# Reciprocal square roots of a hybrid decoder layer: twelve VectorE steps against one VectorE step and a GpSimd power

## Chip, cores and metric

The kernel runs on one core of one Trainium2 chip. The metric is the device time of one execution in microseconds (us). Before the change three runs gave 2449.33, 2453.66 and 2454.43 us, so the median is 2453.66 us. The engines are called PE (TensorE), DVE (VectorE), ACT (ScalarE), POOL (GpSimd) and SP (the engine that starts most DMAs).

## What is computed

One layer for a prompt of 2048 tokens with 16 meta tokens ahead of it, and for 8 single tokens of running sequences. The parts that matter here:

```python
hn = rmsnorm(h, norm1_g)                       # rsqrt per token
q, f, i, g, a, b = split(hn @ w_in)
o, s_new = hgrn2_chunked(silu(q), 1 - f, i, log f)   # 4 heads, gated recurrence
y_hg = rmsnorm(o, hg_onorm_g) * silu(g)        # rsqrt per token and head
glu = a * sigmoid(b)
dw = depthwise_conv(glu, conv_w, 31 taps) + conv_b
y_cv = silu(layernorm(dw))                     # rsqrt per token
h = h + concat(y_hg, y_cv) @ w_out
h = h + square(relu(rmsnorm(h) @ w_up)) @ w_down
y = rmsnorm(h, final_g)                        # rsqrt per token
```

## The kernel before, in words

The prompt is worked on in four quarters of 512 tokens (the meta and sample tokens ride with the first). Every large product is done in three passes (`mm3`, high and low parts of both operands), in matmuls of 128 weights by up to 536 columns. Phase 1 runs, quarter by quarter, the input projection (24 units of 24 or 48 matmuls: columns a and b for the convolution, f, q, g, v for the heads) and the output projection (8 units). Phase 2 is the MLP over two halves. The weights of phase 1 are split into their parts once, by an ACT copy and a POOL subtraction (`split_to`), and are stored and loaded again later.

Beside these units run background tasks, written as Python generators: `x_pair` normalises and transposes two 128-token blocks of the input for the next quarter; `hgrn` does the recurrence of one head and quarter; `conv` starts two `conv_part` tasks for one 128-channel block, of which one adds taps on DVE into a PSUM bank and the other scales taps on ACT and adds them on POOL, until the 31 taps are used up, and the two sums are added; `ln` is the convolution's layer norm; `finish` and `finish_last` do the last norm. This two-sum convolution stands in the kernel before as well as after.

The order of all instructions is fixed when the program is built. `Model` keeps a clock for each engine, `Proxy.call` charges each instruction a cost (for a small DVE step of n elements 68 + 1.1 n ns, for POOL 60 + 2.2 n ns), and `Background.ready` lets a task issue its next step when by those clocks its input is there and the engine is free; for PE that is when the input is ready by the time PE comes to it. Each engine then runs its own list strictly in order and waits on semaphores. So where an engine is later than the planner's clock, whoever is next in line behind it waits.

`rsqrt` is called 49 times: once in `factors` (5 values for each partition), 6 times in `x_pair` (2), 16 times in `hgrn` (4), once in `hgrn_sample_norm` (32), 9 times in `ln_tiles` (2, once 1), 15 times in `finish` (1) and once in `finish_last` (2). All but the last 16 lie in phase 1. It is the bit trick with three Newton rounds: a multiply-add, a shift, an integer multiply-add, and nine more steps, all tiny, all on DVE, each needing the one before. `gap` adds 130 ns to the task's clock between two of them, so that other DVE work is put there. What follows a call: in `hgrn`, four ACT copies scaled by the result (into `on`, which is the tile `KPn`) and then four PE transposes of it; in `x_pair`, `row_bc`, which multiplies the identity by it on DVE (tile `dg`) for PE to spread; in `ln_tiles`, one more DVE step, an ACT normalisation into a `scr` tile and four PE transposes of that; in `factors`, the first two evictions.

In the trace `stat` and `kept` are the tiles of these small values. A row of DVE that writes `ps` from `glu` and `cw` is a convolution tap.

Of the kernel before, what the change touches and what calls it, by code (L numbers as in the profile page):

```python
# [10 lines left out]
I32 = mybir.dt.int32  # L11
U32 = mybir.dt.uint32
AF = mybir.ActivationFunctionType
ALU = mybir.AluOpType
AX = mybir.AxisListType

P = 128
# [11 lines left out]
HALO = TAPS - 1  # L29
DFF = 4096  # L30
EPS = 1e-6
MAGIC = float(0x5F3759DF)
INC = QT + META + NS
QOFF, FOFF, VOFF, GOFF, AOFF, BOFF = 0, 512, 1024, 1536, 2048, 2560

# [64 lines left out]
def _size(ap):  # L100
    n = 1
    for d in ap.shape[1:]:
        n *= d
    return n


class Proxy:
# [3 lines left out]
    def __getattr__(self, f):  # L111
        fn, name, model = getattr(self._eng, f), self._name, self._model

        def call(*args, **kw):
            out = kw.get("out", args[0] if args else None)
            if f == "dma_start":
                n = 4
                for d in out.shape:
                    n *= d
                model.dma(n)  # L120
            else:
                n = _size(out)
                if name == "pe":
                    rhs = kw.get("rhs")
                    if f == "transpose" or rhs.dtype != F32R:
                        cost = max(17 + 0.72 * n, 60.0) if f == "transpose" else max(1.67 * n, 214.0)
                        if n == 1:
                            cost = 425.0
                    else:
                        cost = 2.6 + 0.4167 * n  # L130
                elif name == "act":
                    cost = 130 + 0.8 * n
                    if not isinstance(kw.get("scale", 1.0), float):
                        cost += 100
                elif name == "pool":
                    cost = 60 + 2.2 * n
                elif f == "reciprocal":
                    cost = 60 + 6.3 * n
                elif f in ("bn_stats", "tensor_reduce"):
                    cost = 65 + 1.05 * _size(args[1])  # L140
                elif f in ("tensor_copy", "memset"):
                    cost = 65 + 0.53 * n
                else:
                    cost = 68 + 1.1 * n
                model.op(name, cost)
            return fn(*args, **kw)  # L146

        return call
# [71 lines left out]
def tile_hybrid_step(  # L220
# [6 lines left out]
    V, S, G, T, SP = (Proxy(e, n, model) for e, n in (  # L227
        (nc.vector, "dve"), (nc.scalar, "act"), (nc.gpsimd, "pool"), (nc.tensor, "pe"), (nc.sync, "dma")))
# [9 lines left out]
    def ct(shape, dt=F32, name=None):  # L238
        return const.tile(shape, dt, name=name)
# [8 lines left out]
    c0 = ct([P, HEADS], name="c0")  # L248
    nc1 = ct([P, HEADS], name="nc1")
    stat = ct([P, 104], name="stat")  # L250
    kept = ct([P, 88], name="kept")
    msn = ct([P, 2, 9], name="msn")
    rs2 = ct([P, 2, 9], name="rs2")
# [19 lines left out]
    ps = psum.tile([P, 8, 512], F32, name="ps")  # L273
# [11 lines left out]
    def sc(n):  # L285
        if scols[0] + n > 104:
            scols[0] = 0
        a = stat[:, scols[0]:scols[0] + n]
        scols[0] += n
        return a  # L290

    def keep(n):

        if kcols[0] + n > 88:
            kcols[0] = 0
        a = kept[:, kcols[0]:kcols[0] + n]
        kcols[0] += n
        return a

    def rsqrt(src, n, scale, parts=P, bufs=None):  # L300

        x, a, y = bufs or (sc(n)[:parts], sc(n)[:parts], keep(n)[:parts])
        V.tensor_scalar(x, src, scale, EPS, ALU.mult, ALU.add)
        yield from gap()
        V.tensor_scalar(a.bitcast(I32), x.bitcast(I32), 1, None, ALU.logical_shift_right)
        yield from gap()
        V.tensor_scalar(y.bitcast(I32), a.bitcast(I32), -1.0, MAGIC, ALU.mult, ALU.add)
        yield from gap()
        for _ in range(3):
            V.scalar_tensor_tensor(out=a, in0=x, scalar=-0.5, in1=y, op0=ALU.mult, op1=ALU.mult)  # L310
            yield from gap()
            V.tensor_tensor(a, a, y, ALU.mult)
            yield from gap()
            V.scalar_tensor_tensor(out=y, in0=a, scalar=1.5, in1=y, op0=ALU.add, op1=ALU.mult)
            yield from gap()
        return y

    def gap():
        model.cur.t += 130.0
        yield "dve"  # L320
# [21 lines left out]
    def bank1():  # L342
        got = yield from bank(1)
        return got[0]

    def until(*keys):
        while not all(k in done for k in keys):
            yield "poll"
        model.cur.t = max([model.cur.t] + [done[k] for k in keys])
# [9 lines left out]
    def mix_base(q):  # L359
        return K8 if q == NQ - 1 else 0  # L360

    def hi_lo(dst_hi, dst_lo, src):
        S.activation(dst_hi, src, AF.Copy)
        n = _size(src)
        if n >= 256 and max(model.t["pool"], model.t["pe"]) + 2.2 * n < max(model.t["dve"], model.t["pe"]) + 1.1 * n:
            G.tensor_tensor(dst_lo, src, dst_hi.bitcast(F32), ALU.subtract)
        else:
            V.tensor_tensor(dst_lo, src, dst_hi.bitcast(F32), ALU.subtract)
# [24 lines left out]
    def x_pair(q, pr):  # L393
        t0 = q * QT + pr * 256
        tiles = yield from take(xns, 2)
        yield "sp"
        for i, t in enumerate(tiles):
            SP.dma_start(t[:, 0:D], xp[t0 + i * P:t0 + (i + 1) * P, :])
        yield "act"
        ss = sc(2)  # L400
        for i, t in enumerate(tiles):
            S.activation(junk, t[:, 0:D], AF.Square, accum_out=ss[:, i:i + 1])
        yield "dve"
        r = yield from rsqrt(ss, 2, 1.0 / D)
        yield from row_bc([r[:, i:i + 1] for i in range(2)], bc_t[:, pr])
        yield from region(1, q - 1)
        left = [2]
        for w in range(2):
            bg.add(x_work(q, pr, w, tiles, left), 2.5)
# [146 lines left out]
    def factors(dgs, epilogues):  # L556

        n = META + NS
        yield from take1(dgate)
        yield "dve"  # L560
        r = yield from rsqrt(ss0, 5, 1.0 / D)
        for i in range(4):
            V.tensor_scalar(dgs[:, i], ident, r[:, i:i + 1], None, ALU.mult)
        V.tensor_scalar(dg_t[:n, 0, 0:n], ident[:n, 0:n], r[:n, 4:5], None, ALU.mult)
        yield "pe"
        b, b2 = yield from bank(2)
        for i in range(4):
            T.matmul(ps[:, b, i * P:(i + 1) * P], lhsT=ones, rhs=dgs[:, i], start=True, stop=True)
        T.matmul(ps[:, b2, 0:n], lhsT=ones[:n, :], rhs=dg_t[:n, 0, 0:n], start=True, stop=True)
        dgate.give(0)  # L570
        yield "act"
        S.activation(bc0[:, META:META + QT], ps[:, b, :], AF.Copy)
        S.activation(bc0[:, 0:META], ps[:, b2, 0:META], AF.Copy)
        S.activation(bc0[:, META + QT:INC], ps[:, b2, META:n], AF.Copy)
        banks.give(b, b2)
        done.add(("r0",))
        for i, f in enumerate(epilogues):
            yield "dve"
            f()
            done.add(("first", i))  # L580
# [205 lines left out]
    with tc.manual_schedule():  # L786
        make_identity(nc, ident)
        G.memset(ones, 1.0)

        with ExitStack() as p1:  # L790
            mix_p = p1.enter_context(tc.tile_pool(name="mix", bufs=1))

            def mt(shape, name, dt=F32):
                return mix_p.tile(shape, dt, name=name)
# [19 lines left out]
            aux = mt([P, 96], "aux")  # L814
# [62 lines left out]
            sqs = small[:, 320:352]  # L877
            dws = aux[:, 0:32].rearrange("p (c b) -> p c b", c=NC4)
            ms_ = aux[:, 64:96]
# [178 lines left out]
            def hgrn_sample_norm():  # L1058
                yield from until(*[("hs", h) for h in range(HEADS)])
                yield "dve"  # L1060
                V.tensor_tensor(sqs, osT, osT, ALU.mult)
                yield "pe"
                b = yield from bank1()
                T.matmul(ps[:, b, 0:32], lhsT=ones, rhs=sqs, start=True, stop=True)
                yield "dve"
                r_ = yield from rsqrt(ps[:, b, 0:32], 32, 1.0 / P, bufs=(aux[:, 32:64], sqs, ms_))
                banks.give(b)
                V.tensor_tensor(osT, osT, r_, ALU.mult)
                V.scalar_tensor_tensor(out=ms_, in0=osT, scalar=onorm, in1=sgs, op0=ALU.mult, op1=ALU.mult)
                yield "act"  # L1070
                for h in range(HEADS):
                    s_ = mix_base(0) + h
                    hi_lo(act[:, s_, 0, QT:QT + NS], act[:, s_, 1, QT:QT + NS], ms_[:, h * NS:(h + 1) * NS])
                done.add(("hsn",))
# [630 lines left out]
```

## Time and profile before

| what | before |
|---|---|
| median of three runs | 2453.66 us |
| the profiled execution, its own time | 2447.64 us |
| its span, first to last instruction | 2445.7 us |
| PE busy | 2352.7 us (96%) |
| DVE busy | 1171.4 us (48%) |
| ACT busy | 683.4 us (28%) |
| POOL busy | 520.7 us (21%) |
| mean granted TensorE clock | 0.982 |

The busy share is an average over two phases. PE is close to always busy after about 960 us, so only what happens before that, and the last 46 us, can move the time by much. There the question is which instruction PE waits for, and what that one waited for in its turn. The granted clock is given as a share of 2.4 GHz; 0.50 is the lower level, 1.2 GHz.

### The profile page before, as it was taken

The numbers are of one execution on the slowest core, as the hardware profiler recorded it, in microseconds if no ns is written. First come the engines' busy times: TensorE is split into PE (matmuls) and PEld (weight loads), VectorE is DVE, ScalarE is ACT, GpSimd is POOL, SyncE is SP. The second block draws the span as 40 slices with busy tenths as digits, with TensorE's granted clock in tenths as the row PEclk, the third lists the DMA queues.
The fourth block names the chain that finished last, engine by engine and source line by source line (L and its number), as shares of the span: only waits on it lengthen the run. The fifth ranks groups of instructions, "written<-read, shape, count | busy, mean of one in ns | idle before, by whom it ended". The sixth has DMA issues, their size and how long they took to land.

```text
span 2445.7 us, 31621 instructions
## 1 busy us (share of the span) xinstructions
PE 2352.7 (96%) x13000; PEld 2100.7 (86%) x13000; DVE 1171.4 (48%) x2003; ACT 683.4 (28%) x1239; POOL 520.7 (21%) x326
## 2 busy tenths in 40 slices
PE   8887898989999999999999999999999999999998
PEld 8887777967887788999999999999888888888887
DVE  6798978587659653523323323326722212222225
ACT  6443644463345333212212211213301100100112
POOL 4562414442237112222212212211000000000000
PEclk9889999999999999999999999999999999999999
DMA  9665454944474468644444444448522222222222
GB/s 300 201 215 175 153 192 139 307 165 167 168 248 159 144 233 294 232 155 141 130 150 135 138 147 140 136 153 304 216 94 95 94 98 92 98 92 98 92 93 97
DMA packets 159221, 396.27 MB, mean 162 GB/s; under 512 B 8772, under 2 KB 107657, under 8 KB 125278
## 3 DMA queue, kind: packets, MB, share of 16 engines
q1 hardware_dynamic: 158934, 394.00, 47.5%
q8 instruction: 102, 1.67, 0.3%
q14 instruction: 41, 0.34, 0.0%
q10 hardware_dynamic: 144, 0.26, 0.0%
HBM read 265.91 MB, written 128.79 MB: 161 GB/s over the span
## 4 chain that ended last, share of the span: by engine, by line
PE 73%; DVE 6%; ACT 1%; DMA 1%; issue 0%; POOL 0%; SPq 0%; ACTq 0%; POOLq 0%; DVEq 0%
PE ps L146 73%; DVE ps L146 3%; DVE stat L146 1%; ACT scr L146 0%; DVE kept L146 0%; DMA scr<-xscr 0%; DVE I L146 0%; DMA wsp<-kw 0%; POOL scr L146 0%; DVE act L146 0%; DVE scr L146 0%; DVE glu L146 0%; DVE B L146 0%; DVE xn L146 0%; ACT act L146 0%
## 5 line engine op out<-in xcount | busy, mean ns | idle before, releaser
L146 PE MATMUL ps<-act,wsp 128*128 128x512 f32 (+5 forms) x7704 | 1504.6, 354 | 8.8 <-POOL wsp L146 4.3
L146 PEld LDWEIGHTS ps<-act,wsp 128*128 128x128 f32 x7704 | 1284.4, 191 | 171.2 <-POOL wsp L146 4.9
L146 PE MATMUL ps<-hid,wsp 128*128 128x344 f32 (+4 forms) x3864 | 713.0, 345 | 1.6 <-DMA wsp<-kw 1.6
L146 PEld LDWEIGHTS ps<-hid,wsp 128*128 128x128 f32 x3864 | 646.4, 188 | 64.0 <-issue 1.8
L146 DVE TENSOR_TENSOR acc<-ps,acc 128x1032 f32<-128x1032 f32 (+5 forms) x160 | 162.0, 1013 | 467.4 <-PE ps L146 467.3
L146 POOL TENSOR_TENSOR wsp<-raw,wsp 128x1024 fp32r<-128x1024 f32 (+1 forms) x98 | 235.6, 2404 | 611.4 <-ACT wsp L146 575.8
L146 DVE TENSOR_TENSOR xn<-xn 128x1032 f32<-128x1032 f32 (+3 forms) x68 | 80.3, 1180 | 509.3 <-ACT hid L146 509.3
L146 ACT ACTIVATE xn<-ps 128x1032 f32<-128x1032 f32 (+5 forms) x74 | 69.2, 935 | 835.1 <-PE ps L146 832.3
L146 POOL TENSOR_TENSOR scr<-scr 128x512 f32<-128x512 f32 x172 | 227.8, 1325 | 266.8 <-ACT scr L146 241.8
L146 DVE SCALAR_TENSOR_TENSOR ps<-glu,cw,ps 128x512 f32<-128x512 f32 x292 | 219.5, 752 | 5.8
L146 ACT ACTIVATE wsp<-raw 128x1024 fp32r<-128x1024 f32 (+1 forms) x98 | 101.6, 1037 | 299.8 <-PE ps L146 216.0
L146 DVE TENSOR_TENSOR hid<-xn,hid 128x1032 fp32r<-128x1032 f32 (+3 forms) x68 | 133.5, 1963 | 2.3
L146 ACT ACTIVATE scr<-glu,cw 128x512 f32<-128x512 f32 x188 | 125.7, 715 | 2.0 <-DVE glu L146 2.0
L146 DVE TENSOR_TENSOR scr<-ps,scr 128x512 f32<-128x512 f32 x48 | 32.8, 684 | 81.1 <-DMA scr<-xscr 55.8
L146 ACT ACTIVATE hid<-xn 128x1032 fp32r<-128x1032 f32 (+3 forms) x68 | 69.0, 1015 | 2.2
L146 ACT ACTIVATE junk<-ps 128x128 bf16<-128x128 f32 (+3 forms) x100 | 38.3, 383 | 108.4 <-PE ps L146 95.2
L146 POOL TENSOR_TENSOR fg<-fg 128x512 f32<-128x512 f32 x28 | 36.6, 1307 | 97.7 <-ACT fg L146 97.7
L146 DVE RECIPROCAL I<-B 128x512 f32<-128x512 f32 (+1 forms) x16 | 54.0, 3378 | 0.5
L146 DVE SCALAR_TENSOR_TENSOR stat<-stat,kept 128x4 f32<-128x4 f32 (+4 forms) x144 | 41.8, 291 | 3.3
L146 DVE TENSOR_TENSOR act<-scr,act 128x512 fp32r<-128x512 f32 (+1 forms) x30 | 23.7, 791 | 37.7 <-ACT act L146 37.6
L146 PE MATMUL ps<-ident,scr 128*128 128x128 f32 (+1 forms) x148 | 22.1, 282 | 17.8 <-ACT scr L146 17.8
L146 DVE TENSOR_TENSOR stat<-stat,kept 128x4 f32<-128x4 f32 (+4 forms) x144 | 37.6, 261 | 3.4
(189 smaller groups left out, 1192.1 us busy)
## 6 DMA issues: line engine op xcount, KB each, us to landing
wsp<-kw SPq DMA_DIRECT2D x167, 1024.0 KB, 4.8
kw<-wsp SPq DMA_DIRECT2D x96, 1024.0 KB, 5.6
raw<-in_w_up_dram SPq DMA_DIRECT2D x32, 512.0 KB, 6.5
raw<-in_w_down_dram SPq DMA_DIRECT2D x32, 512.0 KB, 6.0
raw<-in_w_in_dram SPq DMA_DIRECT2D x24, 512.0 KB, 7.9
out_dram<-xn SPq DMA_DIRECT2D x18, 512.0 KB, 4.4
scr<-xscr SPq DMA_DIRECT2D x32, 256.0 KB, 7.2
hscr<-scr SPq DMA_DIRECT2D x32, 256.0 KB, 7.1
```

The costliest lines, as they stand in the source:

```text
L146: return fn(*args, **kw)
```

## The change

`rsqrt` becomes one DVE multiply-add (x = src · scale + EPS) and one POOL `tensor_tensor` with the operation power, whose second operand is a constant tile `mhalf` of -0.5. The eleven steps after the multiply-add are gone, and with them the twelve gaps into which other DVE work was put. The planner gets a cost for the new instruction. The sample norm writes to other scratch tiles. Nothing else is edited; but since the planner's clocks change, the order changes on every engine.

```diff
@@ Proxy.call
+                elif name == "pool" and ALU.pow in args:
+                    cost = 400 + 155 * n
                 elif name == "pool":
                     cost = 60 + 2.2 * n
@@ constants
+    mhalf = ct([P, 32], name="mhalf")
@@ rsqrt
-        x, a, y = bufs or (sc(n)[:parts], sc(n)[:parts], keep(n)[:parts])
+        x, y = bufs or (sc(n)[:parts], keep(n)[:parts])
         V.tensor_scalar(x, src, scale, EPS, ALU.mult, ALU.add)
-        yield from gap()
-        V.tensor_scalar(a.bitcast(I32), x.bitcast(I32), 1, None, ALU.logical_shift_right)
-        yield from gap()
-        V.tensor_scalar(y.bitcast(I32), a.bitcast(I32), -1.0, MAGIC, ALU.mult, ALU.add)
-        yield from gap()
-        for _ in range(3):
-            V.scalar_tensor_tensor(out=a, in0=x, scalar=-0.5, in1=y, op0=ALU.mult, op1=ALU.mult)
-            yield from gap()
-            V.tensor_tensor(a, a, y, ALU.mult)
-            yield from gap()
-            V.scalar_tensor_tensor(out=y, in0=a, scalar=1.5, in1=y, op0=ALU.add, op1=ALU.mult)
-            yield from gap()
+        yield "pool"
+        G.tensor_tensor(y, x, mhalf[:parts, 0:n], ALU.pow)
+        yield "dve"
         return y
@@ start of the schedule
         G.memset(ones, 1.0)
+        G.memset(mhalf, -0.5)
@@ hgrn_sample_norm
-                r_ = yield from rsqrt(ps[:, b, 0:32], 32, 1.0 / P, bufs=(aux[:, 32:64], sqs, ms_))
+                r_ = yield from rsqrt(ps[:, b, 0:32], 32, 1.0 / P, bufs=(aux[:, 32:64], ms_))
```

How the change moves instructions is seen in the engines' lists. The first place is DVE at the second head of the first quarter, where `rsqrt` works on 4 values. Before:

```order
L146 TENSOR_TENSOR V_123<-ps,fg 128x536
L146 TENSOR_SCALAR stat<-stat 128x4
L146 SCALAR_TENSOR_TENSOR ps<-glu,cw,ps 128x512
L146 TENSOR_SCALAR stat<-stat 128x4
L146 SCALAR_TENSOR_TENSOR ps<-glu,cw,ps 128x512
L146 TENSOR_SCALAR kept<-stat 128x4
L146 SCALAR_TENSOR_TENSOR ps<-glu,cw,ps 128x512
L146 SCALAR_TENSOR_TENSOR stat<-stat,kept 128x4
L146 SCALAR_TENSOR_TENSOR ps<-glu,cw,ps 128x512
L146 TENSOR_TENSOR stat<-stat,kept 128x4
L146 SCALAR_TENSOR_TENSOR ps<-glu,cw,ps 128x512
L146 SCALAR_TENSOR_TENSOR kept<-stat,kept 128x4
```

The same place now:

```order
L147 TENSOR_SCALAR ps<-glu,cw,vec 128x512
L147 SCALAR_TENSOR_TENSOR ps<-glu,cw,ps 128x512 x4
L147 TENSOR_SCALAR stat<-stat 128x4
L147 SCALAR_TENSOR_TENSOR ps<-glu,cw,ps 128x512 x2
L147 TENSOR_TENSOR Sg_123<-ps,fg 128x520
L147 SCALAR_TENSOR_TENSOR ps<-glu,cw,ps 128x512 x2
L147 SCALAR_TENSOR_TENSOR xn_90<-xn_91,smp,xn_90 128x128 x8
```

Before, a tap stood behind each of the twelve steps (six steps are shown, the other six go on in the same way). Now only the first step is left, and the taps stand in a row. The state update of the sample tokens (`xn` from `smp`, eight instructions) has come close behind it.

The second place is POOL, at the same head. Now:

```order
L147 TENSOR_TENSOR wsp_88<-raw_86,wsp_88 128x1024
L147 TENSOR_TENSOR scr<-scr 128x512
L147 TENSOR_TENSOR kept<-stat,mhalf 128x4
L147 TENSOR_TENSOR wsp_89<-raw_85,wsp_89 128x1024
L147 TENSOR_TENSOR scr<-scr 128x512
```

The power (`kept` from `stat` and `mhalf`) stands behind a weight split (`wsp`) and a convolution add (`scr`), and ahead of the next weight split.

The third place is PE between the last product with the state (`Sch`) of the third head of the third quarter and the transposes of its normalised output (`KPn`). Before:

```order
L146 MATMUL ps<-Sch,Q_117 128x128
L146 MATMUL ps<-act,wsp_87 128x512 x24
L146 MATMUL ps<-act,wsp_88 128x512 x3
L146 MATMUL ps<-ident,KPn 128x128 x4
L146 MATMUL ps<-ident,xn_92 128x128
```

The same place now:

```order
L147 MATMUL ps<-Sch,Q_119 128x128
L147 MATMUL ps<-act,wsp_88 128x512 x21
L147 MATMUL ps<-ident,KPn 128x128 x4
L147 MATMUL ps<-act,wsp_88 128x512 x3
L147 MATMUL ps<-act,wsp_89 128x512 x3
```

The transposes have moved forward: 21 matmuls of the projection stand ahead of them and not 27. Over the whole program the taps that DVE takes go from 292 to 299 and the POOL adds from 172 to 165.

## Rows read from the trace of the kernel before

**Rows 1.** Busy time by stage: PE, PEld, DVE, ACT, POOL, then granted clock, DMA.

```profile
0.00:420.00 420.00, 362.98 (x2256) 325.87 (x2257) 344.81 (x667) 211.45 (x452) 183.94 (x131) 0.93 0.59 197
420.00:960.00 540.00, 517.46 (x2712) 436.28 (x2711) 352.18 (x712) 228.42 (x481) 174.60 (x127) 0.98 0.60 208
960.00:2400.00 1440.00, 1437.94 (x7763) 1305.64 (x7762) 442.55 (x482) 230.66 (x269) 162.16 (x68) 1.00 0.41 137
```

**Rows 2.** Waits of PE, 0 to 960 us: total us, times, longest us.

```profile
PE ps L146 <- ACT KPn L146: 18.8, 5, 10.6
PE ps L146 <- ACT scr L146: 17.8, 5, 5.6
PE ps L146 <- DVE dg L146: 15.8, 5, 6.9
...
PE ps L146 <- POOL wsp L146: 4.3, 3, 2.0
```

**Rows 3.** Timeline, second head of the first quarter: start us, us, engine, instruction.

```profile
189.20 7.64 PE L146 MATMUL ps<-act,wsp 128*128 128x268 f32 x60
...
190.85 0.19 ACT L146 ACTIVATION_READ_ACCUMULATOR junk<-ps 128x1 f32 x1
...
194.33 1.09 DVE L146 TENSOR_SCALAR stat<-stat 128x4 f32<-128x4 f32 x1
...
197.94 2.34 POOL L146 TENSOR_TENSOR wsp<-raw,wsp 128x1024 fp32r<-128x1024 f32 x1
198.58 1.72 DVE L146 SCALAR_TENSOR_TENSOR stat<-stat,kept 128x4 f32<-128x4 f32 x1
200.22 0.74 DVE L146 SCALAR_TENSOR_TENSOR ps<-glu,cw,ps 128x512 f32<-128x512 f32 x1
...
206.84 0.16 DVE L146 SCALAR_TENSOR_TENSOR kept<-stat,kept 128x4 f32<-128x4 f32 x1
...
207.46 0.99 PE L146 MATMUL ps<-ident,KPn 128*128 128x128 f32 x3 [10.61 <-ACT KPn L146]
```

**Rows 4.** Timeline of PE: the first and the last of twelve long waits.

```profile
68.48 1.23 PE L146 MATMUL ps<-dg,ones 128*128 128x128 f32 x4 [6.95 <-DVE dg L146]
...
748.13 1.12 PE L146 MATMUL ps<-ident,scr 128*128 128x128 f32 x4 [4.40 <-ACT scr L146]
```

**Rows 5.** Busy time by stretch, just behind two of these waits (columns as above).

```profile
207.40:212.00 4.60, 4.54 (x21) 4.32 (x22) 4.38 (x9) 2.48 (x11) 2.56 (x2) 0.50 0.00 0
...
748.10:752.00 3.90, 3.87 (x12) 3.26 (x13) 3.64 (x5) 3.24 (x8) 0.46 (x1) 0.56 0.00 0
```

**Rows 6.** Timeline, third head of the third quarter, where nothing stands between the steps.

```profile
650.26 6.50 PE L146 MATMUL ps<-act,wsp 128*128 128x512 f32 x27
...
652.15 0.37 DVE L146 TENSOR_SCALAR stat<-stat 128x4 f32<-128x4 f32 x2 [3.91 <-ACT junk L146]
...
654.53 1.14 ACT L146 ACTIVATE KPn<-ps,kept 128x128 f32<-128x128 f32 x4 [2.41 <-DVE kept L146]
...
656.61 0.60 PE L146 MATMUL ps<-ident,KPn 128*128 128x128 f32 x4
```

**Rows 7.** Groups of DVE, 0 to 960 us: count, busy us, mean ns, idle before.

```profile
L146 DVE SCALAR_TENSOR_TENSOR stat<-stat,kept 128x4 f32<-128x4 f32 (+3 forms) x96 | 34.3, 357 | 2.2
...
L146 DVE TENSOR_TENSOR stat<-stat,kept 128x4 f32<-128x4 f32 (+3 forms) x96 | 30.1, 314 | 2.2
L146 DVE SCALAR_TENSOR_TENSOR kept<-stat,kept 128x2 f32<-128x2 f32 (+3 forms) x105 | 28.2, 268 | 2.6
...
L146 DVE SCALAR_TENSOR_TENSOR xn<-xn,smp,xn 128x128 f32<-128x128 f32 x32 | 11.7, 438 | 0.0
```

**Rows 8.** Groups of POOL, 0 to 960 us (columns as in the group before).

```profile
L146 POOL TENSOR_TENSOR scr<-scr 128x512 f32<-128x512 f32 x172 | 227.8, 1325 | 266.8 <-ACT scr L146 241.8 <-issue 12.7 <-DVE act L146 2.9
...
L146 POOL MEMSET ss<- 128x5 f32 x1 | 0.1, 104 | 0.0
```

**Rows 9.** Timeline of DVE, the last norm at the end of the program.

```profile
2436.98 0.17 DVE L146 TENSOR_SCALAR stat<-kept 128x2 f32<-128x2 f32 x1
...
2439.61 0.16 DVE L146 TENSOR_TENSOR kept<-kept,rs 128x2 f32<-128x2 f32 x1
```

More of the change, by code (lines that the diff above doesn't have):

```diff
@@ L31 @@
 EPS = 1e-6
-MAGIC = float(0x5F3759DF)
 INC = QT + META + NS
```

## The prediction, made before the changed kernel was run

> **What bounds the kernel now.** I read the busy time by stage first. From 960 to 2400 us PE is busy for 1437.94 of 1440 us at a granted clock of 1.00: nothing on another engine can shorten that stretch. From 0 to 960 us PE is busy for 362.98 + 517.46 = 880.4 us and idle for 79.6 us, and the granted clock is 0.93 and 0.98 [rows 1]. So the change can act there and in the last microseconds.
>
> Next I read whom PE waits for in that stretch. The three longest entries are the scaled copies of a head (`KPn`, 18.8 us), the tiles of the layer norm (`scr`, 17.8 us) and the diagonal of the input norm (`dg`, 15.8 us) [rows 2]. All three come directly behind `rsqrt`. Together they are 52.4 of the 79.6 us, in 15 waits, of which twelve are longer than 2 us (the timeline gives the first and the last of these twelve [rows 4]).
>
> Then I followed one such wait. The squares of the head end at 191.04 us. DVE begins the multiply-add only at 194.33 us, since it is working off its list, and finishes the last step at 207.00 us; PE has 7.64 us of other matmuls in the meantime and then idles for 10.61 us [rows 3]. The twelve steps take 12.7 us there because a tap of 0.74 us stands behind each of them, and because some are drawn out: one that reads two small tiles lasts 1.72 us and ends at 200.30 us, together with the POOL instruction that ends at 197.94 + 2.34 = 200.28 us [rows 3]. Where nothing stands between the steps, the whole chain takes 2.41 us, and PE, with 6.50 us of matmuls in hand, does not wait at all [rows 6].
>
> Behind a long wait PE also runs slowly for a while: 4.60 us at 0.50 (the 1.2 GHz level) after the wait of 10.6 us, 3.90 us at 0.56 after that of 4.40 us [rows 4, 5]. That is a loss of 4.60 · 0.50 = 2.3 us and of 3.90 · 0.44 = 1.7 us. I take 2.0 us for each of the twelve, 24 us in all.
>
> So the chains cost about 52 + 24 = 76 us of phase 1, and that is the most that shortening them can give back there.
>
> **What goes.** In phase 1 there are 32 calls on the small tiles. Three of the five kinds of step that go took 34.3 + 30.1 + 28.2 = 92.6 us of DVE in 297 instructions, of which 9 stay; the other two kinds add to that [rows 7]. So some 90 to 110 us of DVE work in phase 1 disappear. DVE is busy there for 344.81 + 352.18 = 697 of 960 us, and for 82% of the first 420 us [rows 1], and there it is late against the plan. The seven more taps that it now takes cost 7 · 0.74 = 5 us of that.
>
> **What comes.** Each call now waits for one POOL instruction. The trace has no power on POOL. From below, POOL's smallest row of a few columns is 0.10 us, and from above its longest is 2.34 us for 1024 columns [rows 3, 8]; I do not exclude more, which is a rival. The code of the change itself plans 400 + 155 n ns, that is 0.71 us for 2 values and 1.02 us for 4. I take 1.0 us for a head, which lies between the ends, and about 0.1 us for each hand-over.
>
> For a chain with nothing between its steps the new length at a head is: 652.15 - 650.26 = 1.9 us from PE's last state product to the multiply-add, 0.2 us for that, 0.1 + 1.0 + 0.1 us for the power, 0.4 us for the first scaled copy: 3.7 us. PE now has 21 and not 27 matmuls in hand, 21 · 6.50 / 27 = 5.1 us [rows 6]. That leaves 1.4 us, about one POOL add of 1.325 us [rows 8]. So the planner has used up part of the gain by asking for the result sooner: a chain behind one add is just in time, behind two it is late.
>
> **The sum**, against the profiled execution's own time of 2447.64 us:
>
> 1. The wait of 10.61 us. DVE begins its multiply-add no earlier than now, since the list ahead of it is as long. By the new order four taps, one eviction of the size of a tap and eight state updates of 0.44 us follow, 5 · 0.74 + 8 · 0.44 = 7.2 us [rows 3, 7], and PE wants these updates ahead of the transposes. They are done at 194.3 + 0.2 + 7.2 = 201.7 us; PE arrives at about 197.2 us. A wait of 4.5 us is left, 6 us are gained.
> 2. The other 41.8 us of chain waits. The step itself becomes 10 us shorter where taps stood in it, but the start is as late as DVE's list, and the consumers have moved forward. I take half as gained: 21 us.
> 3. The slow stretches behind them go with them, 24 · 27 / 52 = 12 us.
> 4. The 27 us of other waits of PE (79.6 - 52.4) are mostly on DVE, which loses some 90 us of work. I take 4 us as gained, with 0 and 15 us as ends.
> 5. POOL. Some 32 powers of 0.7 to 1.2 us and one on 32 values, 5.4 us by the plan's line, make about 33 us; seven adds of 1.325 us go. POOL is busy for 183.94 + 174.60 of 960 us [rows 1], so its share is no limit, but some nine powers stand ahead of a weight split. PE's waits for these splits are 4.3 us now [rows 2]; nine delays of 1.0 us would make at most 9 us more. I take 4 us lost, with 0 and 9 us as ends.
> 6. The end. From 2436.98 us to 2439.61 us DVE goes through the chain with nothing beside it but 0.5 us of other work: 2.6 us [rows 9]. Now it is 0.2 + 0.1 + 0.7 + 0.1 = 1.1 us, so 1.6 us less (rounded).
> 7. The 15 calls of the MLP phase lie beside PE's 1437.94 of 1440 us [rows 1] and count for nothing; if their cover were gone, they would cost what they cost before or less.
>
> Sum: -6 - 21 - 12 - 4 + 4 - 1.6 = -40.6 us, so 2407 us for an execution like the profiled one. That one is 6 us under the median of the runs shown, 2453.66 us; from the median the sum gives **2413 us**.
>
> GPSIMD Engine Reference in the Trainium skill, section "Instruction dispatch", says that the first call of freshly loaded code on that engine costs about 6 us without an instruction of its own; if that held for the power, the first call, ahead of the first evictions, would be later by that, and the sum would be 2419 us. No row of this trace shows it.
>
> **Rivals.**
>
> *Half of it comes back elsewhere.* While a POOL instruction runs, a small DVE step on SBUF tiles stays open until it ends, as the step of 1.72 us does, whereas a tap, which reads and writes PSUM, keeps its 0.74 us [rows 3]. The powers bring 33 us of POOL time of that kind. In addition DVE's lists are as tight as before, since the planner fills the freed time with taps. Then DVE remains late, the waits appear under other names (the state updates of item 1, the evictions), and of the 27 us of chain waits and the 12 us behind them about half is lost again: 2413 + 20 = 2433 us. For it speaks the wait of 4.5 us in item 1; against it, that 90 us of DVE work are gone for good. The same page of the Trainium skill, section "Specifications", states that the two engines share their SBUF interfaces and that DVE instructions with two SBUF inputs are among those that contend. By that rule this rival is real, and the step of 1.72 us agrees with it.
>
> *The power is the new wait, and the kernel is slower.* In the third head of the third quarter PE has 5.1 us in hand and the chain without the power takes 2.7 us. So from 2.4 us on, for the power with its place in POOL's line, every tight chain makes PE wait and drops its clock. With 4 us there are 32 waits of 1.6 us and 2.0 us of slow clock behind each: 32 · 3.6 = 115 us against the 76 us that go, 2453.7 + 39 = 2493 us. Even is 32 · (w + 2.0) = 76, so w = 0.4 us: 2.8 us for the power and its line. A power of 1.5 us behind one add of 1.325 us is already there. For it speaks that each POOL list holds adds that wait for ACT (241.8 us idle for that [rows 8]), so that a power can stand behind a late add; against it, that POOL is idle for 63% of phase 1.
>
> *Nothing measurable.* The planner moves each consumer forward by as much as the chain becomes shorter, and the lateness of DVE, which causes the waits, stays. Then only the end is gained: 2452 us. The order at the third place speaks for it, the 10 us by which an interleaved chain shrinks against it.
>
> **How the numbers follow.** The forecast gets 0.60, with 2385 to 2428 us as its own range: 2413 less half of items 2 and 3 again plus items 4 at its far end, and plus half of them. Half of it gets 0.20 (2428 to 2447 us), nothing measurable 0.08, slower 0.12. A measurement of this kernel can tell about 0.2%, 5 us, from no change. Faster is 0.60 + 0.20, same 0.08, slower 0.12. The range that leaves out the last two cases is 2382 to 2447 us; its lower end is close to the case in which all 76 + 1.6 us go (2376 us).
>
> **What would show it.** Right: PE's idle time from 0 to 960 us near 50 us, the three entries behind `rsqrt` near 25 us together, a power of 4 values near 1.0 us, the chain at the end shorter by 1.6 us, the stretch from about 960 us on as long as before. Half of it: new entries for `xn`, evictions or `act` in PE's waits. Slower: PE waiting for `KPn` in nearly all 16 heads, ACT waiting for POOL `kept`. The forecast is wrong if the entries behind `rsqrt` stay near 50 us, or if they go and the time stays.

## The result, and the profile after

| what | before | after |
|---|---|---|
| median of the runs beside each other | 2454.05 us (4 runs) | 2411.14 us (4 runs, 2407.99 to 2413.44) |
| the profiled execution, its own time | 2447.64 us | 2407.99 us |
| its span | 2445.7 us | 2406.3 us |
| PE busy | 2352.7 us | 2345.2 us |
| mean granted TensorE clock | 0.982 | 0.987 |

The ratio of the medians is 0.983, with an interval from 0.981 to 0.985: the change makes the kernel faster by 43 us, or 39.6 us between the two profiled executions. The predicted 2413 us was right within the spread of the runs.

Where the time came from is read first in the busy time by stage of the changed kernel (columns as in [rows 1]):

```profile
0.00:420.00 420.00, 384.61 (x2473) 350.63 (x2474) 324.41 (x537) 221.60 (x478) 208.52 (x150) 0.95 0.64 213
420.00:960.00 540.00, 524.65 (x2705) 443.18 (x2704) 307.43 (x499) 225.31 (x469) 187.71 (x144) 0.98 0.62 217
960.00:2400.00 1440.00, 1435.92 (x7827) 1304.54 (x7826) 437.12 (x432) 229.96 (x284) 157.21 (x77) 1.00 0.39 131
```

PE's idle time up to 960 us is now 35.4 + 15.3 = 50.7 us, against 79.6 us before [rows 1]. DVE works 631.8 instead of 697 us in that stretch, POOL 396.2 instead of 358.5 us. That DVE's busy time falls by 65 us and not by the 90 to 110 us of steps that went has two reasons that the rows show: the faster kernel has got further by 960 us (2473 + 2705 matmuls against 2256 + 2712), and some steps last longer (the last section). Behind 960 us there is as little to win as before.

Next, whom PE waits for from 0 to 960 us in the changed kernel (total us, times, longest us):

```profile
PE ps L147 <- DVE I L147: 12.7, 6, 4.5
PE ps L147 <- ACT scr L147: 12.0, 5, 3.1
PE ps L147 <- DVE dg L147: 8.8, 4, 3.2
PE ps L147 <- DVE V L147: 6.5, 2, 5.5
```

`KPn` has left the list, `scr` and `dg` are smaller: 52.4 us behind `rsqrt` [rows 2] became 12.0 + 8.8 = 20.8 us. The wait for the POOL splits (`wsp`, 4.3 us before) is gone too. Two entries grew, both on DVE: `I`, a tile of the recurrence (8.7 us before), and `V` (1.1 us before). Of `V`, 5.5 us are one wait for an eviction that makes a value tile of the recurrence; the other 1.0 us, like the 1.1 us before, is the first norm, which uses the same tile.

The place that the prediction followed step by step, the second head of the first quarter, in the timeline of the changed kernel (start us, duration us, engine, instruction, in brackets the idle time ahead of it and what ended it):

```profile
172.24 0.20 ACT L147 ACTIVATION_READ_ACCUMULATOR junk<-ps 128x1 f32 x1
...
172.47 0.17 DVE L147 TENSOR_SCALAR stat<-stat 128x4 f32<-128x4 f32 x1 [0.58 <-ACT junk L147]
172.72 1.02 POOL L147 TENSOR_TENSOR kept<-stat,mhalf 128x4 f32<-128x4 f32 x1 [6.71 <-DVE stat L147]
...
176.77 1.11 ACT L147 ACTIVATE KPn<-ps,kept 128x128 f32<-128x128 f32 x4
...
179.12 1.70 PE L147 MATMUL ps<-smp,xn 128*128 128x2 f32 x12 [0.39 <-DVE xn L147]
...
180.67 0.64 PE L147 MATMUL ps<-ident,KPn 128*128 128x128 f32 x4
```

Before, the multiply-add began 3.3 us behind the squares and the chain took 12.7 us [rows 3]. Now DVE is not late at all: it stands idle for 0.58 us until the squares end at 172.44 us, and the power is done at 173.74 us, 1.3 us later. The scaled copies start only at 176.77 us, because ACT is working on something else. Even so PE waits 0.39 us where it waited 10.61 us.

The power itself, in the groups of POOL over the whole run (instructions by shape: count, busy us, mean ns of one, then the idle time before them and what ended it):

```profile
L147 POOL TENSOR_TENSOR kept<-stat,mhalf 128x4 f32<-128x4 f32 x16 | 16.3, 1016 | 141.9 <-DVE stat L147 138.2 <-PE ps L147 3.6
L147 POOL TENSOR_TENSOR kept<-stat,mhalf 128x2 f32<-128x2 f32 x15 | 11.0, 734 | 41.5 <-DVE stat L147 41.4
L147 POOL TENSOR_TENSOR kept<-stat,mhalf 128x1 f32<-128x1 f32 x14 | 7.7, 550 | 752.6 <-DVE stat L147 750.6 <-DVE kept L147 2.0
L147 POOL TENSOR_TENSOR aux<-aux,mhalf 128x32 f32<-128x32 f32 x1 | 5.4, 5426 | 17.0 <-DVE aux L147 17.0
```

With 1.18 us for the one call on 5 values, these are about 0.40 us and 0.157 us for each value: the line by which the change's own code plans it. Nearly all of POOL's idle time ahead of them (138.2 of 141.9 us at the heads) was ended by DVE: POOL stood ready, and was not the engine that was late.

### The profile page after: what moved, and what is told of

It is laid out like the page before. It is cut to its first block, busy times and chain, and to the rows that moved or that the text cites. A ratio compares the mean times of both kernels' runs of the same rounds, so it can differ in the third digit from the quotient of the medians.

```text
span 2406.3 us, 31122 instructions
## 1 busy us (share of the span) xinstructions
PE 2345.2 (97%) x13000; PEld 2098.3 (87%) x13000; DVE 1070.1 (44%) x1470; ACT 678.2 (28%) x1232; POOL 553.9 (23%) x370
## 4 chain that ended last, share of the span: by engine, by line
PE 84%; DVE 10%; DMA 2%; ACT 1%; issue 1%; POOL 1%; SPq 0%; POOLq 0%; ACTq 0%; DVEq 0%
PE ps L147 84%; DVE ps L147 4%; DVE I L147 1%; DVE K L147 1%; ACT scr L147 1%; DVE glu L147 1%; DMA raw<-in_w_in_dram 1%; DVE xn L147 1%; DVE scr L147 1%; DVE B L147 0%; DVE kept L147 0%; DVE stat L147 0%; DMA scr<-xscr 0%; POOL scr L147 0%; DMA hscr<-scr 0%
## 5 line engine op out<-in xcount | busy, mean ns | idle before, releaser
L147 POOL TENSOR_TENSOR scr<-scr 128x512 f32<-128x512 f32 x165 | 218.3, 1323 | 161.6 <-ACT scr L147 143.7
L147 POOL TENSOR_TENSOR kept<-stat,mhalf 128x4 f32<-128x4 f32 (+4 forms) x48 | 37.2, 776 | 935.9 <-DVE stat L147 930.1
L147 DVE SCALAR_TENSOR_TENSOR ps<-glu,cw,ps 128x512 f32<-128x512 f32 x299 | 225.3, 753 | 8.7
L147 ACT ACTIVATE scr<-glu,cw 128x512 f32<-128x512 f32 x181 | 120.6, 713 | 7.6 <-DVE glu L147 7.6
L147 PEld LDWEIGHTS ps<-ident,scr 128*128 128x128 f32 (+1 forms) x148 | 18.0, 146 | 15.4 <-ACT scr L147 13.1
```

## The experiments

Two theories stood beside each other. By the first ("chain"), the time was in the length of the chain from the squares to the result. By the second ("load"), it was in the DVE work that goes, for which other tasks' steps stood in line. Rivals on POOL and on the planner came after. Every ratio is to the kernel before, on the same chip, with its 95% interval.

### The power in one group of calls alone

Of the 49 calls of `rsqrt`, f1 changes the 16 in `hgrn`, f2 the 16 in `factors`, `x_pair` and `ln_tiles`; the rest keep the twelve steps.

```diff
+    def rsqrt_pow(src, n, scale, parts=P):
...
+        G.tensor_tensor(y, x, mhalf[:parts, 0:n], ALU.pow)
@@ f1: hgrn
-    rr = yield from rsqrt(ss, 4
+    rr = yield from rsqrt_pow(ss, 4
@@ f2: x_pair (factors and ln_tiles alike)
-    r = yield from rsqrt(ss, 2
+    r = yield from rsqrt_pow(ss, 2
```

> The kernel before, with the power only in the 16 calls of the heads (4 values each). Theory 'load' (DVE's removed work counts most, wherever it is removed): half of the 32 calls of phase 1, about half of the 43 us: 2427 to 2438 us, and PE also waits less for entries that are not behind a head. Theory 'chain': the waits for KPn (18.8 us) and the slow clock behind them go, those for scr and dg stay: 2422 to 2435 us. The two differ in the entries: by 'load' scr and dg shrink as well, by 'chain' they stay at 33 us.

> The kernel before, with the power only in the 16 calls of the input norms and the layer norms. Theory 'load': about half of the 43 us, 2427 to 2438 us, and KPn shrinks too. Theory 'chain': the waits for scr and dg (33.6 us of 52.4) shrink to the 21 us that the changed kernel has, KPn stays at 19 us: 2432 to 2445 us.

Measured: f1 2433.54 us, ratio 0.992 [0.990, 0.994], 20 us less; f2 2425.82 us, 0.988 [0.986, 0.991], 28 us less. PE's waits in f1, 0 to 960 us:

```profile
PE ps L148 <- ACT scr L148: 22.4, 6, 6.5
PE ps L148 <- DVE dg L148: 18.0, 5, 7.1
...
PE ps L148 <- ACT KPn L148: 2.8, 2, 1.9
```

and in f2:

```profile
PE ps L148 <- ACT KPn L148: 14.1, 7, 4.0
PE ps L148 <- ACT scr L148: 13.4, 7, 3.5
PE ps L148 <- DVE dg L148: 8.5, 4, 2.9
```

The entries whose own calls were changed fall most, although DVE lost about as much work from 0 to 960 us in both (663.6 and 663.1 us against 697). For which entry falls, this speaks for the chain, but not cleanly: in f1 `scr` and `dg` did not stay but rose by 6.8 us together, and in f2 `KPn` fell by 4.7 us though no head was changed, which 'load' had expected and 'chain' had not. By the time alone nothing is decided: f1 lies in both expected ranges, f2 below both. The two gains add up to 48 us against 43 us for the whole change, the same within their intervals.

### A short chain with all of DVE's work kept

e1 keeps the twelve steps of the kernel before, but the task gives no turn away between them, so that no tap comes between. (`gap` also stands at two places of the layer norm ahead of its `rsqrt`, which close up as well.) e2 keeps the change, but adds eleven small dependent DVE steps for each call in a task of its own, on which nothing waits.

```diff
@@ e1: gap(), in the kernel before
     model.cur.t += 130.0
-    yield "dve"
+    return
+    yield
@@ e2: rsqrt, in the changed kernel
+    bg.add(idle_steps(min(n, 4)), 6)   # 11 x V.tensor_tensor on idle_t
     yield "pool"
     G.tensor_tensor(y, x, mhalf[:parts, 0:n], ALU.pow)
```

> The kernel before, but the twelve steps of each call stand one behind the other on DVE, with no tap between them; DVE does the same work. Theory 'chain' (the 12 to 18 us from first to last step, caused by the taps between the steps, made PE wait): the chain shrinks to about 2.4 us, so 60% to all of the gain of the change appears: 2412 to 2430 us. Theory 'load' (the 90 to 110 us of DVE work that the change removes made DVE early enough): nothing of that work goes, so at most a quarter of the gain: 2443 to 2456 us.

> The changed kernel, with eleven small DVE steps added for each call that work on a scratch tile of their own and that nothing waits for; they stand among the taps as the removed steps did. Theory 'chain': the result still comes early, little is lost: 2411 to 2425 us. Theory 'load': DVE is as late as before, most of the gain is lost: 2435 to 2456 us.

Measured: e1 2434.67 us, 0.992 [0.990, 0.995], 19 us less; e2 2441.68 us, 0.995 [0.993, 0.996], 12 us less. PE's waits in e1:

```profile
PE ps L146 <- ACT scr L146: 15.1, 4, 5.7
...
PE ps L146 <- DVE dg L146: 9.8, 4, 4.4
...
PE ps L146 <- ACT KPn L146: 1.1, 1, 1.1
```

and in e2, with the group of the added steps behind them (count, busy us, mean ns, idle before):

```profile
PE ps L147 <- DVE I L147: 22.0, 9, 4.9
PE ps L147 <- DVE dg L147: 16.5, 5, 7.1
PE ps L147 <- ACT scr L147: 15.9, 6, 5.8
```

```profile
L147 DVE TENSOR_TENSOR idle_t<-idle_t 128x4 f32<-128x4 f32 (+2 forms) x363 | 83.1, 229 | 10.1
```

In both, `KPn` is down, to 1.1 us in e1 and 0.2 us in e2: the heads need only the short chain. But the time falls by less than half of 43 us: e1 lies between the two expected ranges, e2 in that of 'load'. The steps that do nothing bring the waits for `dg`, `scr` and above all `I` back. So neither theory alone is right: taken at face value, the chain's length is worth some 12 to 19 us, and the rest comes with the DVE work that goes.

The planner puts each of these steps at about 0.07 us, and they take 0.23 us. So e2 could be dear because of the work, or because the plan does not know of it. g2 is e2 with planner costs near the measured ones.

```diff
@@ Proxy.call (g2, e3, e4)
-    cost = 60 + 2.2 * n     # POOL
+    cost = 250 + 2.1 * n
-    cost = 68 + 1.1 * n     # small DVE step
+    cost = 145 + 1.2 * n
+    if "accum_out" in kw:   # ACT
+        cost += 170
```

> The changed kernel with the eleven idle DVE steps per call and with the planner costs near the measured durations; without the idle steps this table gave 2402 us. Theory 'load' (the DVE work itself costs): 25 to 30 us are lost again, 2426 to 2434 us. Theory 'unplanned' (the idle steps cost because the planner took 0.07 us for steps that last about 0.23 us): little is lost, 2402 to 2414 us.

Measured: g2 2416.11 us, 0.985 [0.983, 0.986]. Its partner without the steps is e4 (below), 2402.41 us. So the same steps cost 2441.7 - 2411.1 = 30.5 us under the old costs and 13.7 us under the truer ones. g2 lies 2 us above the range of 'unplanned' and 10 us below that of 'load'. Taken at face value, about half of the load's price is the work, the other half the plan's ignorance of it. Every such edit changes the order on all engines, so I would not split it more finely; how far these splits can be trusted at all is the subject of the end of this section.

### What a longer power would have cost

f4 issues each power three times, the first two to a scratch tile, past the planner; g1 does the same and tells the planner.

```diff
@@ f4: rsqrt
+    for _ in range(2):
+        nc.gpsimd.tensor_tensor(more_t[:parts, 0:n], x, mhalf[:parts, 0:n], ALU.pow)
     G.tensor_tensor(y, x, mhalf[:parts, 0:n], ALU.pow)
@@ g1: f4, and in Proxy.call
-    cost = 400 + 155 * n
+    cost = 3 * (400 + 155 * n)
```

> The changed kernel, in the same order, with each power issued three times (two go to a scratch tile and are unknown to the planner): 2.0 us more for each head, 1.4 us for each norm. By the rival 'the power is the new wait' with its own arithmetic (5.1 us in hand, 3.7 + 2.0 us of chain, a slow clock behind every wait): 32 waits of 0.6 us and 2.0 us of slow clock, 83 us, about 2494 us. If a short wait does not slow the clock and DVE, not POOL, is the late one: 10 to 30 us, 2421 to 2441 us.

> Each power issued three times as in the run of 2465 us, but now the planner is told the threefold cost. If an unplanned delay is what costs (the consumers stand where the result is not yet there), nearly all of the 54 us come back: 2411 to 2428 us. If the longer chain or the 80 us of POOL work themselves cost: 2445 to 2470 us.

Measured: f4 2465.07 us, 1.005 [1.004, 1.006]; g1 2416.53 us, 0.985 [0.983, 0.986]. PE's waits in f4:

```profile
PE ps L147 <- ACT scr L147: 18.6, 9, 4.3
PE ps L147 <- ACT KPn L147: 16.6, 11, 9.0
...
PE ps L147 <- DVE dg L147: 12.0, 7, 3.7
```

and one of the tight heads of f4 in the timeline of PE, with the busy time and granted clock of the stretch around it (columns as in [rows 1]):

```profile
577.79 1.10 PE L147 MATMUL ps<-ident,KPn 128*128 128x128 f32 x4 [0.54 <-ACT KPn L147]
```

```profile
577.70:578.90 1.20, 1.11 (x5) 0.75 (x6) 0.00 (x0) 0.81 (x4) 0.00 (x0) 1.00 0.00 0
```

and PE's waits in g1:

```profile
PE ps L147 <- ACT scr L147: 12.2, 5, 5.4
...
PE ps L147 <- ACT KPn L147: 10.2, 1, 10.2
```

So the rival "slower" is a real mechanism: a chain that is 2.0 us longer at a head without the plan's knowledge gives the whole gain back and more, 54 us; the three entries behind `rsqrt` come to 47.2 us again, against 20.8 in the changed kernel. On a straight line between a head's power of 1.02 us (43 us faster) and of 3.05 us (12 us slower), both kernels would be even near 2.6 us for the power alone; the prediction had said 2.8 for the power and its line. The price that it put on each wait was too high, though, and f4 lies in neither expected range. Its 32 tight chains, each with a wait of 0.6 us and 2.0 us of slow clock, would have added 83 us to the changed kernel, and f4 added 54. (Set against all of the 76 us, as the prediction did it, the same rule gives 2453.7 + 32 · 2.6 - 76 = 2461 us; that this is near f4 is chance, since only 43 of the 76 us had been gained.) The waits at seven tight heads are as long as expected, 0.54 to 0.61 us, but the clock does not fall behind them: the granted clock there is 1.00. The four transposes behind one take 1.10 instead of 0.60 us for another reason: they start 0.26 us apart, as far apart as ACT finishes the four scaled copies that they read. So such a wait costs itself and about 0.5 us at the copies' pace, not 2.0 us of slow clock. The one of 9.0 us lies behind the sample norm, whose three powers on 32 values take 16.3 us. And told to the planner, the same longer chain and the same added POOL work (639 us busy instead of 554) cost 5 us. What decides is how late the result is against the plan, not how long it takes.

### The plan's own part

f3 asks whether the planner's moving the consumers forward ate part of the gain: behind the power it lets the task's clock run on by eleven times 72 ns and a `gap` of 130 ns, 2.2 us in all, without an instruction.

```diff
@@ f3: rsqrt
     yield "dve"
+    for _ in range(11):
+        model.cur.t += 72.0
+        yield from gap()
     return y
```

> The changed kernel, but behind each power the planner lets as much of its own time pass (and as many taps go by) as the eleven steps had taken, without any instruction. DVE's load and the real chain are those of the changed kernel, the result is asked for as late as before. Theory 'load' (and item 2 of the prediction, that the planner used up part of the gain by moving the consumers forward): the waits for scr and dg go down further, 2395 to 2408 us. If the consumers' place does not matter: 2408 to 2415 us. If asking later holds the heads back: 2415 to 2430 us.

Measured: f3 2413.77 us, 0.983 [0.981, 0.985], so no different from the change within the intervals, and in the range of 'does not matter'. That the consumers stand earlier costs nothing that can be measured here.

e3 and e4 give the planner the costs of the diff of g2, in the kernel before and in the changed one; g3 (on e1) and g4 (on the change) use costs halfway between the old and these.

```diff
@@ Proxy.call (g3, g4)
-    cost = 60 + 2.2 * n
+    cost = 155 + 2.15 * n
-    cost = 68 + 1.1 * n
+    cost = 105 + 1.15 * n
+    if "accum_out" in kw:
+        cost += 85
```

> The kernel before with other planner costs, near the measured durations: DVE steps 145 + 1.2 n ns (68 + 1.1 n in the kernel before), POOL 250 + 2.1 n, ACT 170 ns more where it also writes a sum. No instruction is added or removed. Theory 'chain': the chain is as long, but PE is told so and takes it up later; the waits behind it shrink, the work of the heads comes later: 2425 to 2450 us. A third theory, 'plan' (PE waits only because the planner's clock for DVE is too early by 10% to 20%): 2405 to 2425 us, as much as the change gives or more. Theory 'load' gives no time of its own here.

> The changed kernel with the same other planner costs. Theory 'chain': the waits that are left (50 us, now mostly on DVE's recurrence steps and on the layer norm) shrink by a third to a half: 2385 to 2403 us. Theory 'plan': the same, or somewhat more. If the waits that are left have nothing to do with the planner's clock: 2405 to 2416 us.

> The kernel before with the twelve steps in one piece on DVE and planner costs halfway between its own and the measured ones. It tells whether a version without GpSimd comes near. Theory 'load': DVE's 90 to 110 us stay, so at best 10 us better than the 2435 us of the same chain with the old costs: 2424 to 2437 us. Theory 'unplanned': 2405 to 2420 us.

> The changed kernel with the same halfway costs. If the gain of 9 us from the measured costs comes from the costs and not from one lucky order, this lies between the two: 2400 to 2411 us. If orders differ by chance by some 10 us: anything from 2395 to 2420 us.

Measured: e3 2448.62 us, 0.998 [0.996, 0.999], 5 us less; e4 2402.41 us, 0.979 [0.976, 0.981], 9 us under the change; g3 2459.29 us, 1.002 [1.001, 1.003], 25 us worse than e1, where neither theory had it; g4 2398.93 us, 0.978 [0.976, 0.979], 12 us under the change and the fastest of all. So the theory 'plan' does not hold for the kernel before: e3 lies in the range of 'chain'. Truer costs make the changed kernel better twice and the kernel with twelve steps hardly better (e3) or worse (g3 against e1). That g4 is better still than e4 was expected only for the case that orders differ by chance: it lies 1 us under the range for a gain that comes from the costs. The waits of g3 grew at the heads again (`KPn`, 1.1 us in e1) and at places far from `rsqrt` (`xn` and `fg`):

```profile
PE ps L148 <- ACT KPn L148: 12.1, 4, 7.7
PE ps L148 <- DVE xn L148: 9.4, 1, 9.4
...
PE ps L148 <- POOL fg L148: 6.7, 1, 6.7
```

One new order has single waits of 7 to 9 us that another does not have. Differences of 10 to 25 us between kernels of different order, the split between chain and load and the 9 and 12 us of e4 and g4 among them, can therefore hold a share of luck; how large it is stays open. The whole change (43 us) and f4 against g1 (49 us) stand clear of that; for f1 and f2 it is the entries of PE's waits that speak, more than the 20 and 28 us; the split between chain and load doesn't stand clear of it.

## Why the prediction was right

Between the profiled executions the span shrank by 39.4 us. PE's idle time up to 960 us gave 79.6 - 50.7 = 28.9 us, its idle time behind that 13.4 - 10.4 = 3.0 us, and its busy time 2352.7 - 2345.2 = 7.5 us. The terms one by one:

1. *The wait of 10.61 us, 6 us predicted, about 10 measured.* The step that failed is "DVE begins its multiply-add no earlier than now, since the list ahead of it is as long". DVE was not behind but idled ahead of the multiply-add; that this is because the earlier chains were gone from its list is likely, but no run shows it by itself. The state updates that should have made a wait of 4.5 us made one of 0.39. (PE had arrived at 207.46 - 10.61 = 196.85 us [rows 3], not at 197.2; that slip of 0.4 us matters as little as the upper end of the range, which by the sum that it names would be 2429 us.)
2. *The other chain waits, 21 us predicted.* Items 1 and 2 together were to give 27 us; the three entries gave 52.4 - 20.8 = 31.6 us. That their sum would be near 25 us was the first thing to look for, and it is 20.8. That the kind of each entry mattered, the runs show: f1 and f2 take away most of their own.
3. *The slow clock, 12 us predicted.* PE's busy time for the same 13000 matmuls fell by 7.5 us, but not all of that is the clock. Counting half of PE's busy time as lost where the trace's clock record is at 0.50, PE lost 31.0 us up to 960 us before and 27.1 us after, so 3.9 us of the 7.5 are the clock; where the rest comes from stays open. The price of 2.0 us was about right: in the ten such stretches at a wait behind `rsqrt` PE lost 22.6 us before, in the five that are left 8.6 us (one of them stands at a wait for `I` as well). What the prediction left out is that the clock falls at other waits too: there PE lost 8.4 us in three stretches before and 18.6 us in eight after. Two of the eight, at the waits of 5.54 us for `V` and of 4.49 us for `I` (columns as in [rows 1]):

```profile
193.30:200.10 6.80, 6.03 (x28) 6.03 (x29) 6.66 (x9) 0.00 (x0) 0.07 (x1) 0.50 0.83 275
...
766.70:773.50 6.80, 5.60 (x19) 4.94 (x20) 5.57 (x13) 0.80 (x2) 0.00 (x0) 0.50 0.00 0
```

4. *Other waits of PE, -4, and 5. POOL, +4: together 0 predicted, 2.7 us more measured* (27.2 to 29.9 us). The sum is close, the places are not. No weight split is waited for. POOL's price was paid elsewhere, at the very first power, as far as it was paid at all. The timeline of the changed kernel:

```profile
26.93 0.17 DVE L147 TENSOR_SCALAR stat<-ss 128x5 f32<-128x5 f32 x1 [3.95 <-ACT junk L147]
...
29.63 2.38 POOL L147 TENSOR_TENSOR wsp<-raw,wsp 128x1024 fp32r<-128x1024 f32 x1 [7.16 <-ACT wsp L147]
...
32.49 1.18 POOL L147 TENSOR_TENSOR kept<-stat,mhalf 128x5 f32<-128x5 f32 x1
...
33.71 0.87 DVE L147 TENSOR_SCALAR V<-ident,kept 128x128 f32<-128x128 f32 x4 [6.60 <-POOL kept L147]
34.05 1.16 PE L147 MATMUL ps<-V,ones 128*128 128x128 f32 x8 [0.97 <-DVE V L147]
```

   The multiply-add ends at 27.1 us, but POOL's line holds a weight split that waits 7.16 us for ACT, and only then comes the power. DVE idles 6.60 us for it. PE waits 0.97 us here, no more than before (1.08 us: the last step of the old chain had ended with the same split), and then 2.40 us at 37.93 us, for a `glu` tile. In the new order eleven small DVE steps stand ahead of that tile that stood behind it, so the 2.40 us are the power's only in part. That first power began right behind its predecessor and took 1.18 us. GPSIMD Engine Reference in the Trainium skill, section "Instruction dispatch", puts about 6 us on the first call of freshly loaded code; no such gap stands ahead of this power, so the 2419 us of that sentence did not come.
   The waits on DVE for `I` and `V` rose by 9.4 us in all, as the rival "half of it comes back elsewhere" had it, but `POOL wsp` and small entries that shrank make up for most of that. The reason that the rival gave, that powers hold DVE's small steps open, is not what the trace shows (the last section).
6. *The end, 1.6 us predicted, 1.64 measured.* In the timeline of DVE and POOL, the last norm of the changed kernel:

```profile
2399.52 0.17 DVE L147 TENSOR_SCALAR stat<-kept 128x2 f32<-128x2 f32 x1
2399.77 0.70 POOL L147 TENSOR_TENSOR kept<-stat,mhalf 128x2 f32<-128x2 f32 x1 [4.41 <-DVE stat L147]
2400.51 0.16 DVE L147 TENSOR_TENSOR kept<-kept,rs 128x2 f32<-128x2 f32 x1 [0.43 <-POOL kept L147]
```

   From the multiply-add to the first step behind the result it is 0.99 us, before it was 2.63 us [rows 9]. The other 1.4 us behind 960 us were not forecast.
7. *The MLP phase for nothing.* From 960 to 2400 us PE is busy for 1435.92 us, 2 us less than before [rows 1]: nothing was won there.

The tight chain, on which the rival "slower" hung, was worked out as 3.7 us against 5.1 us in hand. In the first head of the third quarter of the changed kernel:

```profile
537.33 5.12 PE L147 MATMUL ps<-act,wsp 128*128 128x512 f32 x21
...
539.46 1.02 POOL L147 TENSOR_TENSOR kept<-stat,mhalf 128x4 f32<-128x4 f32 x1 [21.37 <-DVE stat L147]
540.51 1.14 ACT L147 ACTIVATE KPn<-ps,kept 128x128 f32<-128x128 f32 x4 [1.33 <-POOL kept L147]
...
542.29 0.60 PE L147 MATMUL ps<-ident,KPn 128*128 128x128 f32 x4
```

The first of the four copies is done about 3.6 us behind 537.33 (540.51 us and 0.37 us for the first copy), PE has 5.12 us of matmuls, and the transposes start without a wait. That was right, and f4 shows that the margin was as narrow as said. The prediction's remark that the planner had "used up part of the gain by asking for the result sooner" was no cost: f3. That DVE was the engine to look at was right in kind: by e1 and e2, taken at face value, the chain alone would have given less than half.

So the mechanism was right, the waits behind `rsqrt` and the slow clock behind them, and it gave more than forecast: 31.6 + 14.0 us against 27 + 12. The other waits and the slow clock behind those took 2.7 + 10 us back, where the sum had nothing. That the total comes within 2 us of the forecast, with parts that are off by up to 10 us in both directions, is luck.

## What to carry to other kernels

A chain of tiny dependent steps on a busy in-order engine costs whatever is put between its steps, and its steps delay the other tasks in that engine's line; so one instruction on an idle engine can pay, if what stands ahead of it in that engine's line, at the first use too, fits into the time that the consumer has in hand on the tightest chain. Where a planner fixes the order, give it the new instruction's measured cost: some 2 us for each call that it did not know of cost 54 us, the same told to it cost 5 us. Costs nearer to the measured ones for the instructions around it gave another 9 and 12 us in two runs here, which may in part be a lucky order.

## What was not expected of the hardware

The power on POOL costs 0.55, 0.73, 1.02, 1.18 and 5.43 us for 1, 2, 4, 5 and 32 values in each of 128 partitions, and its first use, the one on 5 values, lies on the line through the others. Some small DVE steps last longer than before; in the changed kernel, DVE from 0 to 960 us,

```profile
L147 DVE COPY kept<-I 128x4 f32<-128x4 f32 x16 | 10.2, 639 | 0.0
...
L147 DVE SCALAR_TENSOR_TENSOR K<-K,B,I 128x16 f32<-128x16 f32 x4 | 8.3, 2063 | 0.0
```

where the same groups had a mean of 229 and 478 ns before. Together that is about 13 us of DVE time, (639 - 229) · 16 + (2063 - 478) · 4 ns, in an engine that lost 65 us. The prediction saw one small step end together with a POOL instruction [rows 3], and these are drawn out in the same way: six of the 16 copies take 1.22 to 2.35 us and end, like all four `K` steps, within 0.04 us of the end of a convolution add or a weight split; the ten others take 0.16 us, and no POOL instruction ran beside them. The old chain's steps had suffered most from this: up to 960 us, 81 DVE steps that ended together with a POOL instruction took 72 us more than the shortest of their form before, 59 us of it in the chains of `rsqrt`; now it is 25 steps and 25 us.

The powers do nothing of the kind. The rival "half of it comes back elsewhere" had counted their 33 us as POOL time that holds DVE open, but of the nine DVE steps on SBUF tiles that began while a power ran up to 960 us, eight took their usual 0.16 to 0.69 us, one of them beside the longest power; the ninth began in a power's last 0.03 us and ended with the add behind it. In the timeline of DVE and POOL of the changed kernel:

```profile
98.35 1.74 POOL L147 TENSOR_TENSOR scr<-scr 128x512 f32<-128x512 f32 x1
98.86 1.25 DVE L147 COPY kept<-I 128x4 f32<-128x4 f32 x1
...
314.19 5.43 POOL L147 TENSOR_TENSOR aux<-aux,mhalf 128x32 f32<-128x32 f32 x1 [16.95 <-DVE aux L147]
...
315.37 0.17 DVE L147 TENSOR_SCALAR stat<-stat 128x4 f32<-128x4 f32 x1 [1.26 <-ACT junk L147]
```

Why an add holds such a step open and a power does not, no run shows. Whether the growing wait for `I` hangs on the drawn-out steps was not tried; the one of 2.58 us at 103.34 us stands right behind two of them.
